# A weight-decomposed low-rank forward pass: the compute rest three pairs later, two loads in halves

## The chip, the cores and the metric

The kernel runs on one core of a Trainium2 chip. The metric is device time in microseconds (us). The kernel before takes 163.12 us, the median of four runs (162.65 to 163.76). The core has a matrix engine (TensorE, PE in the profile; PEld is its weight load), VectorE (DVE), ScalarE (ACT), GpSimd (POOL) and SyncE (SP), each with its own queue of instructions, and 16 DMA engines that move data between the device memory (HBM) and the on-chip memory (SBUF). TensorE writes its results to another on-chip memory (PSUM).

## What is computed

A small weight matrix is built once, and then a long matrix is multiplied by it:

```python
# x: (16, 2048, 256) f32, W: (256, 256), lora_A: (256, 16), lora_B: (16, 256), m: (256,)
W_adapted = W + scale * (lora_A @ lora_B)
W_norm = np.sqrt(np.sum(W_adapted ** 2, axis=0, keepdims=True) + 1e-8)
W_final = W_adapted / W_norm * m
y = x.reshape(-1, 256) @ W_final          # 32768 x 256
```

x is 33.6 MB and y as much; both go through the chip once.

## The kernel before, in words

**Tiling.** The 32768 rows are eight blocks of 4096 rows (4 MB of f32 each). A block is eight chunks of 512 rows (0.5 MB, 4 rows for each of the 128 partitions), and two chunks are a pair, the unit of compute: 64 chunks (`NCH`), 32 pairs (`NPR`). The SBUF holds five blocks (`XBUFS`, `x_bufs`): block b lies in buffer b mod 5, and y is written over x in place. So blocks 5, 6 and 7 can only be loaded once the y of blocks 0, 1 and 2 has been stored.

**One pair.** POOL waits for the load of its chunks and rounds them to bf16 in `xb` (`tensor_copy`, L199). TensorE transposes them in eight steps into `xt_ps` (`turned`, L304). DVE copies the result to `xt` (L240). TensorE multiplies with `w_final`, two times eight matmuls, one set per chunk, into `y_ps` (`product`, L318). ACT copies each chunk from `y_ps` over the chunk's x (L258). TensorE's loop turns pair p + 1 before it multiplies pair p, so the product of a pair waits for the rounding of the next one. `xb`, `xt`, `xt_ps` and `y_ps` have two buffers each.

**Loads.** The list `loads` names chunks as (first, count), and SP issues them in that order (L162 to L172), each with a semaphore of its own. All loads up to chunk 36 are issued at the start. Before the load of chunk 37 SP waits for the store of block 0. Before the load of block 5, that is chunk 40, it waits for the stores 0, 1 and 2: block 0, block 1 and the first half of block 2. Before the last half of block 7 it waits for the second half of block 2. Blocks 5 and 6 are one load each, (40, 8) and (48, 8); block 7 is two, (56, 4) and (60, 4).

**Stores.** The list `stores` has (first chunk, count, chunk at which it is due). ACT issues a store after it has copied the chunk at which it is due (L261 to L267), with a drain and a wait before it. The first phase is stores 0 to 3 (blocks 0 to 2), due at chunks 19 to 24, and four stores of one chunk each, 24 to 27, due at chunk 27. The second phase is the rest of block 3 (28, 4), block 4 (32, 8) and block 5 (40, 8), all due at chunk 47, then block 6 at chunk 55 and the halves of block 7 at 59 and 63.

**The rest.** Before it rounds pair 15 (`REST`), POOL waits until store 2 (`HALF`) has landed, and with it all compute rests:

```python
        if p == REST:
            nc.gpsimd.wait_ge(sem(f"store{HALF}"), 16)
```

A row of a partition in a load or a store is contiguous in HBM and becomes one packet: 32 KB for a whole block, 16 KB for half of one, 4 KB for a single chunk. Loads travel in SP's DMA queue (q1 in the profile), stores in ACT's (q10), and both on the same 16 engines.

Of the kernel before, what the change touches and what calls it, by code (L numbers as in the profile page):

```python
# [11 lines left out]
def kernel(  # L12
# [26 lines left out]
    NBLK = N // BLK  # L39
# [3 lines left out]
    XBUFS = 5  # L43
    CH = DJ // J
    NCH = NBLK * CH
# [2 lines left out]
    PRB = CH // 2  # L48
    NXB = 2

    REST = 15
    IDLE = 8
    NXT = 2
    F8 = 2 * J * P
# [47 lines left out]
    units = [(b * CH, CH) for b in range(NBLK - 1)]  # L102
    units += [(NCH - CH, CH // 2), (NCH - CH // 2, CH // 2)]
    loads = [(0, 2), (2, 2), (4, CH - 4)] + units[1 : XBUFS - 1]


    loads += [((XBUFS - 1) * CH, CH - 3)]
    loads += [(XBUFS * CH - 3 + c, 1) for c in range(3)] + units[XBUFS:]
    load_of = {g: n for n, (g0, cnt) in enumerate(loads) for g in range(g0, g0 + cnt)}


# [2 lines left out]
    F = NBLK - XBUFS  # L114
    G = F * CH
    stores = [(b * CH, CH, 19 + b) for b in range(F - 1)]
    stores += [(G - CH, CH // 2, 24), (G - CH // 2, CH // 2, 24)]
    FIRST = len(stores)
    stores += [(G + c, 1, G + 3) for c in range(4)]
    stores += [(G + 4, CH - 4, 47)]  # L120
    stores += [(b * CH, CH, max(47, (b + 1) * CH - 1)) for b in range(F + 1, NBLK - 1)]
    stores += [(g0, cnt, g0 + cnt - 1) for g0, cnt in units[-2:]]
    HALF = FIRST - 2

# [4 lines left out]
    def sem(name):  # L129
        if name not in sems:  # L130
            sems[name] = tc.alloc_semaphore(name)
        return sems[name]
# [53 lines left out]
    for p in range(NPR):  # L186
        b, c = divmod(p, PRB)
# [3 lines left out]
        if p == 0:  # L191


            nc.gpsimd.wait_ge(sem("dve"), 4)
        if p == REST:
            nc.gpsimd.wait_ge(sem(f"store{HALF}"), 16)
# [57 lines left out]
    for g in range(NCH):  # L254
        b, c = divmod(g, CH)
# [123 lines left out]
```

## Time and profile before

| what | us |
|---|---|
| median of four runs | 163.12 |
| the profiled execution | 162.64 |
| its span, first to last instruction | 161.3 |
| TensorE busy | 97.4 |
| ACT busy | 64.1 |
| POOL busy | 62.7 |
| DVE busy | 44.9 |
| POOL's wait at the rest, ending at 75.9 | 26.2 |
| ACT's last store issue | 134.0 |

Engine times are sums of busy time within the span; they overlap. A line of the timeline gives the start in us, the duration in us, the engine, the source line, the operation, output and input, how many instructions were merged, and in brackets the idle time before it and what ended that. An engine name with a q (SPq, ACTq) is the engine's queue issuing a DMA; the transfer itself runs later on the DMA engines. In the slices of the page a digit is a share in tenths. The granted clock is the share of full speed that TensorE was allowed: 1.0 or 0.5 here, with a mean of 0.842.

### The profile page before, as it was taken

The numbers are of one execution on the slowest core, as the hardware profiler recorded it, in microseconds if no ns is written. First come the engines' busy times: TensorE is split into PE (matmuls) and PEld (weight loads), VectorE is DVE, ScalarE is ACT, GpSimd is POOL, SyncE is SP. The second block draws the span as 40 slices with busy tenths as digits, with TensorE's granted clock in tenths as the row PEclk, the third lists the DMA queues.
The fourth block names the chain that finished last, engine by engine and source line by source line (L and its number), as shares of the span: only waits on it lengthen the run. The fifth ranks groups of instructions, "written<-read, shape, count | busy, mean of one in ns | idle before, by whom it ended". The sixth has DMA issues, their size and how long they took to land. (4 is left out here: it accounts for less than half of the span.)

```text
span 161.3 us, 2012 instructions
## 1 busy us (share of the span) xinstructions
PE 97.4 (60%) x786; PEld 85.1 (53%) x786; DVE 44.9 (28%) x44; ACT 64.1 (40%) x67; POOL 62.7 (39%) x39
## 2 busy tenths in 40 slices
PE   1493996999999600000699939999999990000000
PEld 0253895999998500000689927999799970000000
DVE  0447363353544300000124413454435410000000
ACT  3010464867777520000057742777676772000000
POOL 1274419777673000001938057486758400000000
PEclk9999999999999985555569995999999999555555
DMA  4999999999899999999999999999999999999995
GB/s 154 431 459 459 390 512 398 390 512 398 379 426 447 439 414 431 396 434 423 427 428 430 432 447 422 407 449 422 427 479 406 439 455 398 433 471 398 410 431 215
DMA packets 4356, 67.42 MB, mean 418 GB/s; under 512 B 625, under 2 KB 642, under 8 KB 1666
## 3 DMA queue, kind: packets, MB, share of 16 engines
q1 hardware_dynamic: 2160, 33.82, 49.2%
q10 hardware_dynamic: 2194, 33.59, 48.8%
q14 instruction: 2, 0.02, 0.0%
HBM read 33.85 MB, written 33.55 MB: 418 GB/s over the span
## 5 line engine op out<-in xcount | busy, mean ns | idle before, releaser
L258 ACT COPY x_sb<-y_ps 128x1024 f32<-128x1024 f32 x64 | 62.2, 1014 | 62.1 <-PE y_ps L318 61.4
L199 POOL CAST xb<-x_sb 128x2048 bf16<-128x2048 f32 x32 | 60.2, 1893 | 63.3 <-DMA out_dram<-x_sb 26.2
L318 PE MATMUL y_ps<-w_final,xt 128*128 128x256 bf16 x512 | 65.3, 283 | 1.8 <-PEq L293 1.6
L240 DVE COPY xt<-xt_ps 128x1024 f32<-128x1024 f32 x32 | 39.2, 1225 | 76.6 <-PE xt_ps L304 76.6
L318 PEld LDWEIGHTS y_ps<-w_final,xt 128*128 128x128 bf16 x512 | 51.8, 102 | 9.8 <-issue 2.5
L304 PE MATMUL xt_ps<-identity,xb 128*128 128x128 f32 x264 | 37.6, 290 | 27.8 <-PEq L293 27.8
L304 PEld LDWEIGHTS xt_ps<-identity,xb 128*128 128x128 f32 x264 | 32.3, 150 | 30.0 <-issue 29.6
L285 PE MATMUL y_ps<-sq,ones 128*128 128x256 f32 x4 | 2.1, 674 | 1.6 <-DVE sq L225 1.6
L274 PE MATMUL y_ps<-identity,a_nat 128*16 128x128 f32 x2 | 0.6, 396 | 3.6 <-DMA a_nat<-in_lora_A_dram 3.6
L250 ACT ACTIVATE norm<-y_ps,eps_col 128x256 f32<-128x256 f32 x1 | 0.5, 474 | 5.3 <-PE y_ps L285 5.3
L285 PEld LDWEIGHTS y_ps<-sq,ones 128*128 128x128 f32 x4 | 1.2, 324 | 2.3 <-DVE sq L225 2.1
L248 ACT ACT_TABLE_LOAD x1 | 1.3, 1283 | 2.4 <-issue 2.4
L205 POOL MEMSET xb<- 128x2048 bf16 x1 | 1.8, 1804 | 0.7 <-PE xt_ps L304 0.7
L274 PEld LDWEIGHTS y_ps<-identity,a_nat 128*16 128x16 f32 x2 | 0.1, 90 | 3.6 <-issue 3.6
L233 DVE RECIPROCAL rnorm<-norm 128x256 f32<-128x256 f32 x1 | 1.7, 1737 | 0.0
L227 DVE COPY m_all<-y_ps 128x256 f32<-128x256 f32 x1 | 0.4, 424 | 3.3 <-PE y_ps L290 3.3
L290 PE MATMUL y_ps<-m_row,ones 1*128 1x256 f32 x2 | 1.2, 710 | 0.0
L216 DVE CAST b_bf<-b_nat 16x256 bf16<-16x256 f32 x1 | 0.3, 281 | 3.0 <-DMA b_nat<-in_lora_B_dram 3.0
L278 PE MATMUL y_ps<-b_bf,aT 16*128 16x256 bf16 x2 | 0.6, 404 | 0.7 <-DVE aT L218 0.7
L221 DVE SCALAR_TENSOR_TENSOR wa<-y_ps,w_nat 128x512 f32<-128x512 f32 x1 | 0.7, 692 | 0.8 <-PE y_ps L278 0.8
L290 PEld LDWEIGHTS y_ps<-m_row,ones 1*128 1x128 f32 x2 | 0.5, 308 | 0.7 <-issue 0.7
L230 DVE TENSOR_TENSOR wam<-wa,m_all 128x256 f32<-128x256 f32 x2 | 0.8, 436 | 0.0
(13 smaller groups left out, 3.3 us busy)
## 6 DMA issues: line engine op xcount, KB each, us to landing
x_sb<-in_x_dram SPq DMA_DIRECT2D x5, 4096.0 KB, 29.0
out_dram<-x_sb ACTq DMA_DIRECT2D x5, 4096.0 KB, 22.5
out_dram<-x_sb ACTq DMA_DIRECT2D x5, 2048.0 KB, 27.3
x_sb<-in_x_dram SPq DMA_DIRECT2D x3, 2048.0 KB, 33.7
x_sb<-in_x_dram SPq DMA_DIRECT2D x1, 2560.0 KB, 45.0
x_sb<-in_x_dram SPq DMA_DIRECT2D x2, 1024.0 KB, 6.2
out_dram<-x_sb ACTq DMA_DIRECT2D x4, 512.0 KB, 45.9
x_sb<-in_x_dram SPq DMA_DIRECT2D x3, 512.0 KB, 19.1
```

What stands on the lines that cost most here:

```text
L199: nc.gpsimd.tensor_copy(out=xb_bufs[p % NXB][:], in_=x_bufs[b % XBUFS][:, 2 * c * J : 2 * (c + 1) * J, :],).then_inc(sem("rounded"), 1)
L205: nc.gpsimd.memset(xb_bufs[NPR % NXB][:], 0.0).then_inc(sem("rounded"), 1)
L221: nc.vector.scalar_tensor_tensor(out=wa[:], in0=ab_ps, scalar=float(scale), in1=w_nat[:], op0=ALU.mult, op1=ALU.add).then_inc(dv, 1)
L230: i = nc.vector.tensor_mul(out=wam[:, t], in0=wa[:, t], in1=m_all[:])
L233: nc.vector.reciprocal(out=rnorm[:], in_=norm[:]).then_inc(dv, 1)
L240: nc.vector.tensor_copy(out=xt_bufs[p % NXT][:].rearrange("p r t -> p (r t)").bitcast(FP32), in_=xt_ps[p % 2][:],).then_inc(sem("copied"), 1)
L248: nc.scalar.activation(out=warm[:], in_=eps_col[:], func=AF.Sqrt)
L258: nc.scalar.copy(out=x_bufs[b % XBUFS][:, c * J : (c + 1) * J, :], in_=y_ps[g % 2][:]).then_inc(sem("room"), 1)
L285: i = nc.tensor.matmul(n2_ps, ones[:], sq[:, t, :], start=(t == 0), stop=(t == KC - 1))
L290: nc.tensor.matmul(mb_ps, ones[0:1, :], m_row[:], start=True, stop=True).then_inc(pe, 1)
L304: i = nc.tensor.transpose(xt_ps[p % 2][:, j * P : (j + 1) * P], xb_bufs[p % NXB][:, j, :].bitcast(FP32), identity[:],)
L318: i = nc.tensor.matmul(y_ps[h][:, j, :], xt_bufs[p % NXT][:, r : r + P, t], w_final[:, t, :], start=(t == 0 and (j % (J // 2)) == 0), stop ...
```

## The change

Three numbers and one list change. The rest moves from before pair 15 to before pair 18, so pairs 15, 16 and 17 are computed ahead of it. The loads (40, 8) and (48, 8) become four loads of four chunks, so that with block 7 all loads from chunk 40 on are halves of blocks; each has a semaphore of its own, and POOL waits for each before its first pair. The first three stores of the second phase become due at chunk 53 instead of 47. The bytes moved, the conditions under which SP may issue the loads, and all the instructions of TensorE, DVE and POOL stay; SP issues two DMAs more, and ACT issues three stores after six more copies.

```diff
-    REST = 15
+    REST = 18
...
-    loads += [(XBUFS * CH - 3 + c, 1) for c in range(3)] + units[XBUFS:]
+    loads += [(XBUFS * CH - 3 + c, 1) for c in range(3)]
+
+    loads += [(g0, 4) for g0 in range(XBUFS * CH, NCH, 4)]
...
-    stores += [(G + 4, CH - 4, 47)]
-    stores += [(b * CH, CH, max(47, (b + 1) * CH - 1)) for b in range(F + 1, NBLK - 1)]
+    stores += [(G + 4, CH - 4, 53)]
+    stores += [(b * CH, CH, max(53, (b + 1) * CH - 1)) for b in range(F + 1, NBLK - 1)]
```

Here `XBUFS * CH` is 40, `NCH` is 64, `G` is 24, `F` is 3 and `NBLK` is 8.

## The prediction

> **What bounds the kernel now.** I read the page first, then the transfers by queue in short stretches, then the timeline of each engine around the two store phases.
>
> The head of the page, with the share of the DMA engines in 40 slices:
>
> ```profile
> span 161.3 us, 2012 instructions
> DMA  4999999999899999999999999999999999999995
> GB/s 154 431 459 459 390 512 398 390 512 398 379 426 447 439 414 431 396 434 423 427 428 430 432 447 422 407 449 422 427 479 406 439 455 398 433 471 398 410 431 215
> HBM read 33.85 MB, written 33.55 MB: 418 GB/s over the span
> ```
>
> The DMA engines are full from the second slice to the last but one. In the trace's packet records a 32 KB packet takes 1.21 to 1.22 us and a 16 KB one 0.61 us, reading or writing, which is 27 GB/s on each of 16 engines, 432 GB/s; stretches of loads alone, stores alone and both give 425 to 433. So the end is set by bytes, and only two things can move it: a moment with no transfer outstanding, or packets that move more slowly. TensorE, busy for 97.4 us, ends its work at 133 us, 28 us before the end.
>
> The place to look at is where the loads end. Queues in 114 to 115.5 us, and in 115.5 to 117 us (packets, MB, share of 16 engines; q1 carries loads, q10 stores):
>
> ```profile
> q1 hardware_dynamic: 41, 0.67, 105.2%
> q10 hardware_dynamic: 8, 0.00, 0.3%
> ```
>
> ```profile
> q10 hardware_dynamic: 37, 0.61, 94.5%
> q1 hardware_dynamic: 17, 0.03, 5.7%
> ```
>
> From 114 us only loads are left, and they end on the engines between 115.52 and 116.73 us (packet records; 15 engines by 116.2, one straggler at 116.73). The next stores take over on each engine at once. They were issued here:
>
> ```profile
> 57.73 4.24 ACTq L149 DMA_DIRECT2D out_dram<-x_sb  x4
> ...
> 110.57 1.93 ACT L258 COPY x_sb<-y_ps 128x1024 f32<-128x1024 f32 x2 [0.69 <-PE y_ps L318]
> 112.61 1.36 ACTq L149 DMA_DIRECT2D out_dram<-x_sb  x3
> ```
>
> The issue at 112.61 is the one due at chunk 47. It came 4.1 us before the last load packet ended; its first packet started at 115.52. That is the slack which the change spends.
>
> What releases the compute after the rest, on POOL, which rounds x for TensorE:
>
> ```profile
> 75.92 3.73 POOL L199 CAST xb<-x_sb 128x2048 bf16<-128x2048 f32 x2 [26.17 <-DMA out_dram<-x_sb]
> ...
> 94.41 5.60 POOL L199 CAST xb<-x_sb 128x2048 bf16<-128x2048 f32 x3 [5.56 <-DMA x_sb<-in_x_dram]
> ...
> 105.35 3.73 POOL L199 CAST xb<-x_sb 128x2048 bf16<-128x2048 f32 x2 [1.59 <-DMA x_sb<-in_x_dram]
> ```
>
> The rest ends at 75.9 us with the store of half of block 2; then blocks 5 and 6 are waited for until 94.4 and 105.3 us.
>
> **The change, part by part.**
>
> *Rest at pair 18.* Pairs 15 to 17 move ahead of the rest. Their chunks 30 to 35 have landed by 49.5 us. A pair takes 2.62 us on TensorE (28.41 to 31.03), so 7.9 us; ScalarE copies nothing from 57.7 to 62.0 while it issues four stores, so the work ends near 69 us, or near 74 if the clock is at half and a pair takes 5.3. Both are inside the idle stretch that ends at 75.9, so the cost is nothing; without that cover it would be up to 7.9 us. The gain is nothing too: what is late next is pair 19 (load of chunk 39, landed at 83.4) and then pair 20, which waits for block 5 anyway. DMA is full throughout, so earlier compute buys no bytes.
>
> *Blocks 5 and 6 in halves.* Two more issues on SP, 0.3 to 1.3 us each as the rows there are, at 76 to 82 us, with over 20 us of loads and stores queued: nothing (if that cover were gone, 2.6 us). POOL has two more waits. Packets become 16 KB, at 0.61 us twice against 1.21: nothing, at most 0.2 us over 8.4 MB by the 429 against 432 GB/s of the mixed stretches. What changes is sharing. The four single-chunk stores have 4 KB packets, and the engines alternate one packet of each queue: in 83 to 104 us, 256 load packets of 32 KB started and 241 of 4 KB. With 16 KB loads the alternation goes twice as fast. At 83.0 us 440 of the 4 KB packets were left, 27.5 per engine; at 0.61 + 0.16 us a turn they are through at 104.2 instead of 113.7.
>
> *Second store phase due at chunk 53 instead of 47.* Three DMA issues (1.36 us of ScalarE's queue) move past six copies; those copies lose that wait, and chunk 54 takes it; (48, 8) and later follow far ahead of need. The question is when chunk 53 is done. It needs the load of chunks 52 to 55. Total bytes are the same, so loads end on the engines at 115.5 to 116.7 again. Behind that load stand 16 packets of 16 KB per engine, 9.8 us: it ends on the straggler at 116.73 - 9.8 = 106.95. Its semaphore follows by 0.5 us (block 6: 104.79 to 105.29) to 1.0 (last load: 116.73 to 117.71): 107.6. The lower bound is 105.3, where block 6 landed whole. From landing to the end of that pair's copies I use the same stretch for block 1, which landed at 23.67:
>
> ```profile
> 23.73 5.57 POOL L199 CAST xb<-x_sb 128x2048 bf16<-128x2048 f32 x3 [5.11 <-DMA x_sb<-in_x_dram]
> 25.77 1.06 PE L304 MATMUL xt_ps<-identity,xb 128*128 128x128 f32 x8 [1.25 <-PEq L293]
> 26.66 1.91 PE L318 MATMUL y_ps<-w_final,xt 128*128 128x256 bf16 x16
> 28.41 1.04 PE L304 MATMUL xt_ps<-identity,xb 128*128 128x128 f32 x8
> 29.29 1.91 PE L318 MATMUL y_ps<-w_final,xt 128*128 128x256 bf16 x16
> 30.36 1.93 ACT L258 COPY x_sb<-y_ps 128x1024 f32<-128x1024 f32 x2 [0.69 <-PE y_ps L318]
> ```
>
> Cast, turn, the product before, the next turn, the product, two copies: 32.29, and 0.11 for drain and wait (112.50 to 112.61) make 32.40, which is 8.7 us after landing. So the stores are issued at 107.6 + 8.7 = 116.3 us, 3.7 us later than now and when most engines have just run dry.
>
> *From issue to first packet.* Bounds: 1.0 us on empty engines (0.90 to 1.91 at the start), 2.9 us on busy ones (112.61 to 115.52). I take 1.2, since the engines will be nearly empty: 117.5. The engines stand still for 1.3 to 2 us, but the straggler, which sets the end (last packet 160.82, the others 159.4 to 160.4), only from 116.73: 0.8 us. The Trainium skill ("DMA: Bandwidth & Descriptors", section Latency and other measured facts) gives about 0.6 us to the first byte of such a DMA; by it the straggler would lose 0.2 us and the change would not be measurable. The rows here are longer in every case, 1.0 and up.
>
> *Clock.* After the rest TensorE will have idle stretches of about 3 us ahead of pairs 19 and 20. What such a one does is seen at 96 us, after 2.67 us of idle:
>
> ```profile
> 96.45 1.61 PE L304 MATMUL xt_ps<-identity,xb 128*128 128x128 f32 x8 [2.67 <-PEq L293]
> 97.85 3.08 PE L318 MATMUL y_ps<-w_final,xt 128*128 128x256 bf16 x16
> ```
>
> Pair 19 then cost 4.3 us instead of 2.62, with the granted clock at 0.5 from 96.8 to 100.2. After the change a half lands every 8 x 0.77 = 6.2 us and needs 5.24, so about 1 us per half is regained, and a slip of 1.7 at pair 20 is made good at chunk 53; one of 3.5 (two such windows) leaves 1.75. I add 0.3. The skill's "TensorE: Matmul & The Clock Gate" (section Why this matters for your kernels) asks for no idle over about 3 us between bursts of matmuls, a rule against loads that gate compute like this; had its slow window to be paid in full, the sum would be 1.7 higher, but idle TensorE time here is cover.
>
> *Sum.* 0 + 0 + 0.8 + 0.3 = 1.1 us. The profiled execution took 162.64 us (span 161.3 and 1.3 around it), 0.5 under the median of four; it would become 163.7, and the median 163.12 + 1.1 = 164.2. Ends: landing at 105.3 and 1.0 us of latency give 115.0, in time, so nothing, and below it -0.3 if the quiet 4 KB mix ends sooner; a slip of 1.75 and 2.9 us of latency give 116.3 + 1.75 + 2.9 - 116.73 = +4.2.
>
> **The rivals.**
>
> *In time (not slower).* Chunks 52 to 55 land 1 us or more earlier, because the 4 KB stores take fewer turns than one in two, so the issue comes by 115.3 and its first packet by 116.5. For it: block 6 landed at 105.3 today, with the same bytes ahead of it. Against: that needed the 4 KB stores to last until 113.7, and the pairs of packets counted speak for one to one. It decides at an issue at 115.7, and gives 162.8 to 163.5.
>
> *A wider hole.* TensorE comes out of two slow windows still behind, or the first packet needs 2 to 2.9 us: 165 to 167.3. For it: every issue on busy engines took 2.7 us or more (45.49 to 48.18 too). Against: those waited behind packets already in flight.
>
> *Faster.* Fewer mixed packets move more quickly. The whole loss in mixed stretches that the change touches is 3 GB/s in 432 over 34 us, 0.24 us; the dip at 46.5 to 49 us (0.5 us) is untouched. So there is no 0.8 us to win: 162.9 at best but for scatter.
>
> *The change doesn't do what it says.* Pairs 15 to 17 might not fit before the rest. They would then run at 78 to 88 us, still before pair 20 can start: no difference in time.
>
> **How the numbers follow.** A hole of 0.5 to 1.8 us: 0.55. In time: 0.20. Wider: 0.20. Faster: 0.05. A measurement tells about 0.5% (0.8 us) from no change. Of the first, 0.40 lies above it and 0.15 below; with the wider hole slower is 0.60, the same 0.36 (0.15 + 0.20 + 0.01), faster 0.04. The range goes from 163.0 (0.1 under the median; leaves out the fast case and part of "in time") to 166.0 (leaves out the upper half of the wider hole), at most 0.2 in all.
>
> **What would show it.** Stores of the second phase issued at 116 to 117 us; q10 empty from about 104 us; a slice near 117 us with DMA visibly under full for the first time; pairs 15 to 17 cast before 60 us; POOL waits for loads in steps of about 6 us from 89 us on; everything after the hole shifted by it. I am wrong if the issue stands before 115 us, if the engines' rate changes in a stretch where both queues have work, or if the tail after the last load is longer than 44 us.

## The result, and the profile after

The changed kernel takes 163.67 us (median of 43 runs, 162.78 to 164.54), the kernel before 163.09 us (69 runs, 162.37 to 163.84). The ratio is 1.0036 with a 95% interval of 1.0026 to 1.0047: slower, by 0.6 us (0.4 to 0.8). That is the direction that was forecast, at about half of the 1.1 us, and under the 0.5% that the chances took as their bound. Here and below a ratio is taken over all the runs and can differ in the fourth figure from the quotient of the two medians, and the kernel before was timed anew beside each group of experiments, so that its median stands at 162.92 to 163.09.

The page of the changed kernel (profiled execution 163.87 us, span 162.6):

```profile
span 162.6 us, 2015 instructions
DMA  4999998998999999899999999999699999999997
GB/s 165 430 445 452 435 468 387 452 452 387 441 357 492 395 460 433 372 423 428 413 432 456 401 425 459 427 411 439 270 387 452 492 405 395 500 395 395 443 395 323
```

One slice that was full before is not: the 29th, 113.8 to 117.9 us, with a 6 and 270 GB/s. The queues show what happens around it, first in 104.8 to 115.5 us, then in 116.2 to 117.6 (packets, MB, share of 16 engines; then issues), then in 117.6 to 119:

```profile
q1 hardware_dynamic: 316, 4.65, 101.6%
q10 hardware_dynamic: 1, 0.00, 0.0%
```

```profile
DMA packets 4, 0.00 MB, mean 0 GB/s; under 512 B 4, under 2 KB 4, under 8 KB 4
...
q1 hardware_dynamic: 4, 0.00, 0.2%
issues: line engine op xcount, KB each, median us to landing
out_dram<-x_sb ACTq DMA_DIRECT2D x1, 4096.0 KB, 16.4
out_dram<-x_sb ACTq DMA_DIRECT2D x1, 2048.0 KB, 6.3
```

```profile
q10 hardware_dynamic: 46, 0.75, 128.9%
```

The store queue has nothing to move from 104.6 us on (last 4 KB packet in the packet records: 104.57). The loads go on alone at full rate and run out; between 116.2 and 117.6 no packet with data starts on any of the 16 engines (the four packets in that stretch are a few bytes each), while the next stores have just been issued. The last load packet ended at 116.80, and the first store packet started at 117.64. Then stores alone. ACT's timeline gives the issue, and the copies of the three pairs that moved ahead of the rest:

```profile
57.44 3.98 ACTq L151 DMA_DIRECT2D out_dram<-x_sb  x4
61.47 1.93 ACT L260 COPY x_sb<-y_ps 128x1024 f32<-128x1024 f32 x2 [4.13 <-issue]
...
67.98 1.93 ACT L260 COPY x_sb<-y_ps 128x1024 f32<-128x1024 f32 x2 [1.34 <-PE y_ps L320]
...
114.76 1.93 ACT L260 COPY x_sb<-y_ps 128x1024 f32<-128x1024 f32 x2 [0.69 <-PE y_ps L320]
116.80 1.82 ACTq L151 DMA_DIRECT2D out_dram<-x_sb  x3
```

The early pairs end at 69.9 us, inside the idle stretch. The stores due at chunk 53 are issued at 116.80 instead of 112.61. POOL's timeline shows the rest and the steps of the halves:

```profile
57.23 1.89 POOL L201 CAST xb<-x_sb 128x2048 bf16<-128x2048 f32 x1 [2.09 <-PE xt_ps L306]
76.33 1.89 POOL L201 CAST xb<-x_sb 128x2048 bf16<-128x2048 f32 x1 [17.20 <-DMA out_dram<-x_sb]
83.52 1.89 POOL L201 CAST xb<-x_sb 128x2048 bf16<-128x2048 f32 x1 [5.30 <-DMA x_sb<-in_x_dram]
89.59 3.73 POOL L201 CAST xb<-x_sb 128x2048 bf16<-128x2048 f32 x2 [4.18 <-DMA x_sb<-in_x_dram]
...
107.55 3.73 POOL L201 CAST xb<-x_sb 128x2048 bf16<-128x2048 f32 x2 [1.97 <-DMA x_sb<-in_x_dram]
```

The wait at the rest is 9 us shorter (17.20 against 26.17), and two waits on loads follow at once, 5.30 and 4.18. TensorE's work was moved to an earlier place and nothing came of it.

### The profile page after: what moved, and what is told of

Read it like the earlier page. It is cut to its first block, busy times and chain, and to the rows that moved or that the text cites. A ratio compares the mean times of both kernels' runs of the same rounds, so it can differ in the third digit from the quotient of the medians.

```text
span 162.6 us, 2015 instructions
## 1 busy us (share of the span) xinstructions
PE 100.9 (62%) x786; PEld 87.1 (54%) x786; DVE 44.9 (28%) x44; ACT 64.3 (40%) x67; POOL 62.6 (39%) x39
## 5 line engine op out<-in xcount | busy, mean ns | idle before, releaser
L320 PE MATMUL y_ps<-w_final,xt 128*128 128x256 bf16 x512 | 67.3, 288 | 4.9 <-PEq L295 4.8
L320 PEld LDWEIGHTS y_ps<-w_final,xt 128*128 128x128 bf16 x512 | 52.5, 103 | 14.1 <-issue 5.9
L242 DVE COPY xt<-xt_ps 128x1024 f32<-128x1024 f32 x32 | 39.2, 1225 | 73.5 <-PE xt_ps L306 73.5
L306 PE MATMUL xt_ps<-identity,xb 128*128 128x128 f32 x264 | 38.9, 296 | 18.0 <-PEq L295 18.0
L306 PEld LDWEIGHTS xt_ps<-identity,xb 128*128 128x128 f32 x264 | 33.6, 155 | 20.6 <-issue 20.2
L238 DVE TENSOR_TENSOR w_final<-wam,rnorm 128x256 bf16<-128x256 f32 x2 | 0.8, 422 | 0.0
```

The source lines that it names most:

```text
L238: i = nc.vector.tensor_mul(out=w_final[:, t], in0=wam[:, t], in1=rnorm[:])
L242: nc.vector.tensor_copy(out=xt_bufs[p % NXT][:].rearrange("p r t -> p (r t)").bitcast(FP32), in_=xt_ps[p % 2][:],).then_inc(sem("copied"), 1)
L306: i = nc.tensor.transpose(xt_ps[p % 2][:, j * P : (j + 1) * P], xb_bufs[p % NXB][:, j, :].bitcast(FP32), identity[:],)
L320: i = nc.tensor.matmul(y_ps[h][:, j, :], xt_bufs[p % NXT][:, r : r + P, t], w_final[:, t, :], start=(t == 0 and (j % (J // 2)) == 0), stop ...
```

## The experiments

The theory is the hole: the stores of the second phase come after the loads have run out. Its rivals: *sharing*, that 16 KB loads as such cost, by more packets and more turns for the 4 KB stores; and *compute*, that the rest at pair 18 costs, by TensorE's slow clock after it. Every edit is against the changed kernel unless it says "before". In all of them the second phase means the first three stores of that phase.

### The due chunk alone taken back

```diff
-    stores += [(G + 4, CH - 4, 53)]
-    stores += [(b * CH, CH, max(53, (b + 1) * CH - 1)) for b in range(F + 1, NBLK - 1)]
+    stores += [(G + 4, CH - 4, 47)]
+    stores += [(b * CH, CH, max(47, (b + 1) * CH - 1)) for b in range(F + 1, NBLK - 1)]
```

> The changed kernel with the second store phase due at chunk 47 again; rest at 18 and the halves stay. Hole theory: chunk 47 is done three pairs of 2.62 us earlier, so the stores are issued near 116.8 - 7.9 = 108.9 us, the loads never run out alone, and the time is that of the kernel before, 0.0 us to it within 0.3. Sharing theory (the halves cost, by more packets and more turns for the 4 KB stores): still about 0.6 us slower than before. Compute theory (slow clock after the rest at 18 costs): still 0.6 us slower.

Measured: 163.07 us against 163.09, ratio 1.0002 (0.9988 to 1.0017). The issue came 0.8 us before the expected 108.9:

```profile
108.08 1.33 ACTq L151 DMA_DIRECT2D out_dram<-x_sb  x3
```

So with the rest at 18 and the halves kept, the whole loss is gone. Sharing and compute fall as the cause.

### Only one small store taken back

```diff
-    stores += [(G + 4, CH - 4, 53)]
+    stores += [(G + 4, CH - 4, 47)]
```

> The changed kernel with only the store of chunks 28 to 31 due at chunk 47 again, 2 MB or 4.9 us of transfers; the two large ones stay due at 53. Hole theory: these 4.9 us begin or wait in the queue before the loads end at 115.8 and cover the engines past 117.6, when the others' first packets are there; 0.0 us to the kernel before within 0.3. If it is not the hole but the later issue as such (order of transfers, later end of the large stores), 0.4 to 0.6 us slower.

Measured: 162.97 us against 163.09, ratio 1.0003 (0.9985 to 1.0021). ACT's issues and the share of the DMA engines:

```profile
108.64 0.34 ACTq L151 DMA_DIRECT2D out_dram<-x_sb  x1
116.73 0.86 ACTq L151 DMA_DIRECT2D out_dram<-x_sb  x2
```

```profile
DMA  4999999999899999899999999999999999999995
```

The two large stores are issued as late as in the changed kernel (116.73), and the 29th slice is a nine again: 2 MB in the queue at the right moment are enough. It is not the later issue that costs, it is the empty queue.

### The due chunk one pair earlier, and one pair later

```diff
-    stores += [(G + 4, CH - 4, 53)]
-    stores += [(b * CH, CH, max(53, (b + 1) * CH - 1)) for b in range(F + 1, NBLK - 1)]
+    stores += [(G + 4, CH - 4, 51)]
+    stores += [(b * CH, CH, max(51, (b + 1) * CH - 1)) for b in range(F + 1, NBLK - 1)]
```

and the same with 55. With 55 the store of block 6, due there too, is issued together with the three.

> The changed kernel with the second phase due at chunk 51, one pair of 2.62 us earlier: issue at 114.2, first packets when the loads end at 115.5 to 116.7. Hole theory: no hole, 0.0 us to the kernel before within 0.3, so that the step lies between chunk 51 and 53. Sharing and compute theories: 0.6 us slower still.

> The changed kernel with the second phase due at chunk 55: one pair, 2.62 us, later. Hole theory: issue at 119.4, first packets at 120.3, so the hole grows by 2.6 us and so does the time: 0.6 + 2.6 = 3.2 us slower than before (1.9%). Sharing and compute theories: no change to the changed kernel, 0.6 us slower than before.

Measured for 51: 162.99 us against 162.92, ratio 1.0006 (0.9992 to 1.0019), no hole: the first store packet started at 116.10, as the first engines ran out of loads. For 55: 166.63 against 163.09, ratio 1.0217 (1.0192 to 1.0242), 3.5 us; 3.2 were expected. The issue of each, and the DMA row of the second:

```profile
113.85 3.11 ACTq L151 DMA_DIRECT2D out_dram<-x_sb  x3
```

```profile
119.15 3.12 ACTq L151 DMA_DIRECT2D out_dram<-x_sb  x4
```

```profile
DMA  5999989989899899899999999999199899999997
```

The 6 has become a 1. One pair earlier costs nothing that these runs can tell, one pair later costs nearly 3 us more: the step lies just where the loads end.

### One part alone on the kernel before

The due chunk alone on before:

```diff
-    stores += [(G + 4, CH - 4, 47)]
-    stores += [(b * CH, CH, max(47, (b + 1) * CH - 1)) for b in range(F + 1, NBLK - 1)]
+    stores += [(G + 4, CH - 4, 53)]
+    stores += [(b * CH, CH, max(53, (b + 1) * CH - 1)) for b in range(F + 1, NBLK - 1)]
```

> The kernel before with only the second store phase due at 53. Its copies of chunks 52 and 53 end at 120.8 us, so the issue falls at 120.9 and the first packet at 121.8, and with the loads out at 115.8 to 116.7 the hole theory expects the end 5.1 us later for the straggler and 6 for the rest: 5 us slower (3%). Sharing theory: whole loads, nothing changes, 0.0.

Measured: 167.97 us against 162.92, ratio 1.0309 (1.0277 to 1.0341), 5.05 us; 5 were expected. A slice of the DMA row is empty:

```profile
120.74 1.82 ACTq L149 DMA_DIRECT2D out_dram<-x_sb  x3
```

```profile
DMA  4999989899999999999999999999089989999997
```

The halves alone on before:

```diff
-    loads += [(XBUFS * CH - 3 + c, 1) for c in range(3)] + units[XBUFS:]
+    loads += [(XBUFS * CH - 3 + c, 1) for c in range(3)] + [(g0, 4) for g0 in range(XBUFS * CH, NCH, 4)]
```

> The kernel before with only blocks 5 and 6 in halves. Hole theory: chunk 47 comes somewhat earlier, no hole, 0.0 us within 0.3. Sharing theory: 0.6 us slower, since here alone the halves act. In either case the 4 KB stores should be through at about 104 us instead of 113.7.

Measured: 163.06 us against 162.92, ratio 1.0003 (0.9987 to 1.0019). The 4 KB stores are through at 104.04 us, as expected, and it costs nothing.

The rest alone on before:

```diff
-    REST = 15
+    REST = 18
```

> The kernel before with only the rest moved to pair 18. Hole theory: pair 20 still waits for block 5 at 94.4, chunk 47 is done at 112 to 114 with a slow clock at the start of that stretch, first packets by 115 to 116: 0.0 to 0.3 us slower. Compute theory: 0.6 us slower, since here alone the rest acts.

Measured: 162.98 us against 162.92, ratio 1.0008 (0.9993 to 1.0023). TensorE's clock was at half from 91.8 to 102.1 us in this execution, and the issue at 113.67 was still in time.

So of the three parts only the due chunk costs: alone 5 us. The halves give most of it back, because chunk 53 no longer waits for a whole block: the issue moves from 120.74 to 116.80, and to 115.83 and 117.20 in the two runs below that have the rest at 15 and so differ from this one in the halves alone.

### The rest back at 15, the other two parts kept

```diff
-    REST = 18
+    REST = 15
```

> The changed kernel with the rest before pair 15 again; halves and due 53 stay. Hole theory with the clock as second term: pairs 15 to 17 run at 78 to 88 us and keep TensorE's clock up, pair 20 follows without a pause, and TensorE reaches product 26 at 112.9 instead of 113.7; issue at 116.0 to 116.3 instead of 116.8, so the hole is 0.5 to 0.8 us shorter and the kernel 0.0 to 0.3 us slower than before. If the clock plays no part: issue at 116.8 and 0.6 us slower. If pairs 15 to 17 were worth having early: issue later than 116.8 and more than 0.6 us slower.

Measured: 163.48 us against 163.09, ratio 1.0023 (1.0000 to 1.0046); the issue at 115.83. This interval holds both what the clock theory and what its rival expected. Timed a second time:

> The changed kernel with the rest before pair 15 again, timed once more, since its first interval (0.00 to 0.46% over before) did not separate it from the changed kernel (0.26 to 0.47%). Clock theory: issue between 115.8 and 116.3 and 0.0 to 0.3 us over before; without a part of the clock, 0.6 us over before. The time again first packet + 46.15.

Measured: 163.67 us against 163.05, ratio 1.0040 (1.0017 to 1.0063); the issue at 117.20, outside the window that the clock theory gave. Together the two say that the rest at 18 or 15 makes no difference that these runs can tell. Here are both executions, POOL's cast of chunks 52 to 55 and ACT's issue:

```profile
107.15 3.73 POOL L201 CAST xb<-x_sb 128x2048 bf16<-128x2048 f32 x2 [1.75 <-DMA x_sb<-in_x_dram]
...
115.83 1.82 ACTq L151 DMA_DIRECT2D out_dram<-x_sb  x3
```

```profile
108.53 3.73 POOL L201 CAST xb<-x_sb 128x2048 bf16<-128x2048 f32 x2 [1.74 <-DMA x_sb<-in_x_dram]
...
117.20 1.81 ACTq L151 DMA_DIRECT2D out_dram<-x_sb  x3
```

From cast to issue it is 8.68 and 8.67 us. What differs is when the load landed: 1.4 us later in the second execution. There the load's semaphore got its 16 increments, one per engine, fifteen of them between 106.09 and 106.95 and the last at 108.48: one slow engine held the load back.

### Further executions of the two kernels

> Another look at the kernel before. In the four traces with a hole the device time stood 46.1 to 46.2 us after the first packet of the second store phase; here there is no hole, and the end is set by the one slow DMA engine. If the profiled execution of before was a fast one by 0.45 us because that engine and the loads were early, a more usual look (163.0 to 163.2) shows the loads' last packet and the last store packet some 0.4 us later than 116.7 and 160.8.

> Another look at the changed kernel. Hole theory: time = first packet of the second store phase + 46.15 within 0.1, wherever the issue falls in this execution (116.0 to 117.5), with about 0.85 us from issue to packet. The slow clock windows lie elsewhere in each execution, so the issue should differ from 116.80.

> A third look at the changed kernel, with the same expectation: time = first packet + 46.15 within 0.1.

This execution of before took 163.07 us, the one behind the prediction 162.64. Its last load packet ended at 117.76 (then 116.73) and its last store packet at 161.39 (then 160.82): later by 1.0 and 0.6, where 0.4 each was expected. The second and third execution of the changed kernel took 163.37 and 163.54 us; POOL's cast of chunks 52 to 55 and ACT's issue in each:

```profile
107.63 3.73 POOL L201 CAST xb<-x_sb 128x2048 bf16<-128x2048 f32 x2 [1.72 <-DMA x_sb<-in_x_dram]
...
116.30 1.90 ACTq L151 DMA_DIRECT2D out_dram<-x_sb  x3
```

```profile
107.81 3.73 POOL L201 CAST xb<-x_sb 128x2048 bf16<-128x2048 f32 x2 [1.95 <-DMA x_sb<-in_x_dram]
...
116.48 1.82 ACTq L151 DMA_DIRECT2D out_dram<-x_sb  x3
```

All seven executions with a hole, in the order of their issue (packet records and device times):

| kernel | issue | first packet | device time | time less issue |
|---|---|---|---|---|
| rest 15, first | 115.83 | 116.67 | 162.89 | 47.06 |
| changed, second | 116.30 | 117.14 | 163.37 | 47.07 |
| changed, third | 116.48 | 117.33 | 163.54 | 47.06 |
| changed, first | 116.80 | 117.64 | 163.87 | 47.07 |
| rest 15, second | 117.20 | 118.05 | 164.28 | 47.08 |
| due 55 | 119.15 | 119.99 | 166.18 | 47.03 |
| before, due 53 | 120.74 | 121.59 | 167.86 | 47.12 |

The end follows the issue one for one, at 47.03 to 47.12 us. From the first packet it is 46.19 to 46.27 us; the expected 46.15 within 0.1 held in the three executions for which it was set (46.21 to 46.23). By this sum and the median of before, 163.09, an issue at 116.0 is where it begins to cost; 113.85 (due 51) is safe, and no profile has an issue between 113.85 and 115.83.

None of these kernels is faster than the kernel before: every one without a hole takes what it takes.

## Why the prediction was right or wrong, point by point

*Bytes set the end.* Right. TensorE's last product ended at 132.0 us, and the 133 that the prediction gives it is the end of ACT's last copy, which changes nothing. Each execution without a hole comes out at the time of before, whatever was moved inside.

*Rest at pair 18: nothing.* Right, alone (1.0008, interval through 1) and with the rest of the change. The cover held: the early pairs ended at 69.9, where 69 was worked out, and POOL then stood at loads.

*Halves: nothing by themselves, but the 4 KB stores through at 104.2.* Right; 104.57, and 104.04 with the halves alone. One reading under it was off: in 83 to 104 us of the kernel before, 241 load packets of 32 KB and 236 store packets of 4 KB started, not 256 and 241; that is still one to one.

*Chunks 52 to 55 landed at 107.6, the issue 8.7 us later at 116.3.* Right. They landed at 107.50, 107.57 and 107.75 in three executions; the issue came at 116.80, 116.29 and 116.48.

*Clock: 0.3 us.* The sort of thing was right, its use was small. In the first execution the clock was granted at 0.5 from 73.5 to 83.8 and from 90.6 to 97.4 us, and from cast to issue it took 9.25 instead of 8.67 us. TensorE was still behind there when the load of chunk 53 landed: from 91.6 us to the issue it had no idle time, while in the second execution it stood idle three times between 89 and 117 us. Two stretches of the first and then of the second execution (start and end, length, PE busy with the instructions in brackets, PEld, DVE, ACT, POOL; granted clock, share of the DMA engines, GB/s):

```profile
90.00:97.50 7.50, 5.87 (x28) 4.91 (x29) 1.23 (x1) 1.50 (x2) 5.10 (x3) 0.54 0.99 422
97.50:107.00 9.50, 9.50 (x89) 8.82 (x88) 4.64 (x4) 6.41 (x8) 5.74 (x4) 1.00 1.03 436
```

```profile
90.00:97.50 7.50, 5.69 (x51) 4.83 (x48) 2.45 (x2) 4.19 (x6) 5.13 (x3) 1.00 1.02 434
97.50:107.00 9.50, 8.21 (x74) 7.46 (x75) 3.68 (x3) 5.68 (x7) 6.02 (x4) 1.00 1.01 429
```

In the second and third execution nothing of it was left by chunk 53, and moving the rest, which keeps the clock up from 82 us on, made no measurable difference. The rule of the Trainium skill against long idle between bursts of matmuls ("TensorE: Matmul & The Clock Gate", section Why this matters for your kernels) agrees with the first execution: the clock fell to half at 90.6 us, in an idle stretch of 3.25 us that ended at 91.63. A slow window paid in full, as worked out from the row at 96 us, would have put 1.7 us on the sum; at most 0.6 was seen, in one execution of three.

*From issue to first packet 1.2 us, 0.8 us for the straggler.* This is the step that was mis-sized. Three things went into it. First, the latency on empty engines was 0.84 to 0.85 us in all seven executions, not 1.2: 0.36 too much. The Trainium skill's 0.6 us ("DMA: Bandwidth & Descriptors", section Latency and other measured facts) is nearer to it than the 1.2 that I took. The lower bound of 1.0, from the first small loads, is nearer still, and the 2.9 us on busy engines was no guide at all. Second, I measured the hole against where the straggler stood in one execution of before, which was 0.45 us under the median now known (162.64 against 163.09), and added the difference to a median. A time counted from the issue to the end would have avoided that. Third, and the other way, the tail after a hole is slower than I had it, by 0.2 us (below). 1.1 - 0.36 - 0.45 + 0.2 = 0.5, against 0.6 measured. The first and third terms are measured in each trace; the second rests on two executions of before, so that this splitting is worked out and not shown. The mechanism was right; the third error took back part of the first two, and that the forecast came no further off is in part luck.

*The rivals.* "In time" was to be decided at an issue at 115.7; the table puts the point at 116.0. The changed kernel lies close beyond it, with issues from 116.30 to 116.80 in three executions. Its runs spread a little wider (162.78 to 164.54) than those of the kernel before (162.37 to 163.84); that the spread of the issue is the reason is plausible and not shown. A wider hole was not seen in the changed kernel, and the rows on which it stood do not carry over: with loads still under way the wait from issue to first packet was as short as 1.7 us (rest 18 alone). "Faster" was not seen in any of the kernels.

*The signs.* The issue, the empty store queue, the slice under full, the early casts (done by 59.1 us) and POOL's steps of about 6 us came as listed. One sign of being wrong came true as well: the tail after the last load was to be at most 44 us, and it was 45.3 (116.80 to 162.14). It was set too tight to tell anything, since the kernel before has 44.1 (116.73 to 160.82); of the 45.3 us the hole is 0.8.

*The chances.* 0.60 on slower by over 0.5% was too much; the 0.36% measured belongs to "within 0.5%", which had 0.36. The range of 163.0 to 166.0 held the result, but it also held the time of the kernel before, so that it says little.

## What to carry to other kernels

Where the DMA engines are full from end to end, read the moments at which one queue hands over to the other: find when the old queue's last packet ends and when the new queue's transfers are issued, and keep the difference at more than the latency. A due point moved past it costs one for one, a small transfer already waiting covers it, and work moved earlier on TensorE earned nothing here. And count such a time from the late event to the end, not as a difference to one profiled execution.

## What the runs showed of the hardware that was not expected

- From the issue of a store of 128 rows of 16 KB to its first packet: 0.84 to 0.85 us in the seven executions whose loads had ended by then. With loads still in flight it was 1.7 to 3.4 us in the seven without a hole: 1.65 (rest 18 alone), 2.25 (due 51), 2.91 and 2.68 (the two of before), and 3.4 in the three whose loads went on for over 10 us after the issue. In the first four, nearly all the first store packets start within 0.03 us of the end of a load packet, as the loads run out, although the 4 KB store packets had ended at least 1.0 us earlier. So the wait was short only where the loads were about to end; what sets the 3.4 us was not tried.
- After a hole all engines start within 0.16 us of each other and stay so: the last ends 0.45 to 0.50 us after the median engine in those seven, 0.9 to 2.3 us in the seven without a hole. In step they are a little slower: a 32 KB store packet between 125 and 150 us takes 1.2208 to 1.2219 us on average in the seven with a hole and 1.2149 to 1.2164 in the seven without, 0.5% or 0.2 us over the 43.7 us of the tail. Why was not tried.
- One engine held a load of 2 MB back by 1.5 us (its increment of the semaphore at 108.48, the other fifteen by 106.95), and with it everything that waits for the load. Which engine it is the traces do not say.
